# Queries of the dilated layer turned on VectorE and moved through DRAM instead of transposed on TensorE

## The chip, the cores and the metric

One NeuronCore of one Trainium2 chip runs the whole program. The metric is device time in microseconds; the kernel before takes 861.87 us (median of three runs, 861.83 to 862.84). Engines are named as the profile names them: PE is TensorE (PEld its weight loads), DVE is VectorE, ACT is ScalarE, POOL is GpSimd, SP is SyncE, whose queue starts nearly all DMAs.

## What is computed

Two layers on x of 512 tokens by 1024 features, float32. Each: RMS norm, one input projection, attention in 16 heads of 64, a SiLU gate, an output projection, a residual add. Layer A attends in three groups of dilation per head, merged by their softmax denominators; layer B attends in a neighbourhood of a token grid.

```python
def mixer_a(hn, w_in, w_out, q_gain, k_gain, t5_bias):
    proj = hn @ w_in
    qkv = proj[..., :n_qkv].reshape(b, s, N_DIL_GROUPS, 3, N_HEADS, HEAD_DIM)
    gate = proj[..., n_qkv:]
    for g, (window, dilation) in enumerate(DILATED_PAIRS):
        q = rms_norm(qkv[:, :, g, 0], q_gain[g])
        k = rms_norm(qkv[:, :, g, 1], k_gain[g])
        v = qkv[:, :, g, 2]
        o, lse = dilated_group_attention(q, k, v, t5_bias[...], dilation, reach)
    alpha = jax.nn.softmax(jnp.stack(lses), axis=0)
    y = jnp.sum(alpha[..., None] * jnp.stack(outs), axis=0)
    return (y * jax.nn.silu(gate)) @ w_out
```

Layer A's scores need queries and keys with the head's features on the partitions; the projection leaves them with tokens on the partitions. So they have to be transposed.

## The kernel before

Products in float32 are made of three matmuls each: a value is split into a high part (`wh`, `hn_h`, `q0h`, `k0h`) and a low part (`wl`, `hn_l`, `q0l`, `k0l`), and `mm3` adds high by high, high by low and low by high. Weights come from DRAM in loads of 512 KB (`wraw`, three buffers, line 175). ScalarE casts the high part of 512 columns (`wh`, line 127), VectorE or GpSimd subtracts (`wl`, line 131); four buffers of each, so a split runs four weight tiles ahead. A weight tile feeds 12 matmuls of 512 columns.

Layer A is worked in eight chunks `hc` of two heads. `main_a` issues, per chunk, the projection `rawk` (keys and values of groups 1 and 2; eight weight tiles, 96 matmuls), `rawq` (queries of all groups and key of group 0; 96 matmuls), the values of group 0 (`v0_a`, 24) and the gate (`gate_a`, 24). Each projection lands in four PSUM banks (`acc`), which ScalarE takes out scaled (line 428); GpSimd squares, VectorE sums, a reciprocal root is computed, VectorE scales (line 284; for `rawq` held back until after the gate's product, line 458).

The attention of a chunk is a side stream laid between the projections of the next chunk. TensorE's order is written by the program (`manual_schedule`): `run` alternates the main stream with the side stream, and a side step is emitted when an estimated clock passes a due time (`yield 1200`, `yield "wait", key, delay`). The other engines' orders are made by a planner from the same program. `later_on` puts DMA starts at due times of the same clock, and `keep_in_program_order` fixes them in SP's queue. SP waits in order: a DMA that waits for data or for a buffer holds all behind it.

Per chunk, the side stream is: `k_a` (two groups of four 128x128 transposes, line 210), `q_a` (four groups: queries of the three groups of dilation and the key of group 0), `v_a` (one), then `attn_a`: scores `log` of half the tokens (u = 0), the products with v of the chunk before (`weigh`, tile `o`, called through `pending`), scores of the other half (u = 1). The probabilities are turned by VectorE in 32x32 blocks (`turner.put`, line 636) and sent through DRAM in 256 KB pieces (`td` written at line 645, `pt` read at line 649).

In TensorE's order, counted in projection matmuls from the start of the next chunk's `rawk`: q groups at 24, 30, 36 and 42, the `vt` group at 48, scores at 60, products `o` at 72, end of `rawk` at 96, second scores at 129, k groups at 165 and 171, end of `rawq` at 192.

Of the kernel before, what the change touches and what calls it, by code (L numbers as in the profile page):

```python
# [13 lines left out]
F32 = mybir.dt.float32  # L14
# [28 lines left out]
def tile_hybrid_encoder(  # L43
# [44 lines left out]
    make_identity(nc, ident)  # L88
    ones = cp.tile([P, S], F32R, name="ones")
    nc.vector.memset(ones.bitcast(F32), 1.0)  # L90
# [174 lines left out]

    def squares(raw, ss, i, ns):
        sq = wk.tile([P, 512], F32, tag="sq", name="sq")[:, : ns * 64]
        nc.gpsimd.tensor_mul(sq, raw[:, i, : ns * 64], raw[:, i, : ns * 64])  # L268
# [6 lines left out]
    def head_norm(raw, ss, ns, held):  # L275


        rs = wk.tile([P, 32], F32, tag="rs", name="rs")
        rsqrt(nc.vector if ns == 8 else nc.gpsimd, rs[:, : 4 * ns], ss[:, : 4 * ns], 4 * ns, 1.0 / DH)

        def scale():
            for i in range(4):
                v = raw[:, i, : ns * 64].rearrange("p (a b) -> p a b", b=64)
                m = nc.vector.tensor_mul(
                    v, v, rs[:, i * ns : (i + 1) * ns].unsqueeze(2).to_broadcast([P, ns, 64])
                )
# [58 lines left out]
    for _ in range(9):  # L345
        nc.tensor.matmul(busy, ones[:, :P], ones, start=True, stop=True)
    wsteps = steps()
# [61 lines left out]
    rk = wk.tile([P, 4608], F32, tag="rawk", name="rawk", bufs=1)  # L409

    def project_qk(n, ns, key, hc, guard, first=False, **kw):

        box = []

        def evac(i, acc):
            if not box:
                q = key == "rawq"
                if q:
                    box.append(wk.tile([P, 4, n], F32, tag="rawq", name=key, bufs=1))
                else:  # L420
                    o = 4 * n * (hc % (2 if n == 512 else 3))
# [3 lines left out]
            if first:  # L425
                nc.scalar.copy(raw[:, i, :], acc[:, :n])
                return
            nc.scalar.activation(raw[:, i, :], acc[:, :n], AF.Copy, scale=rs_n[:, i : i + 1])  # L428
            squares(raw, ss, i, ns)

        tile_of = lambda hn: lambda k, i: hn[:, k, P * i : P * (i + 1)]
        yield from project(tile_of(hn_h), tile_of(hn_l), n, evac, guard, **kw)
        raw, ss = box
        if first:
            st["first"] = raw, ss
            return
        normed(raw, ss, ns, key, hc)

    def normed(raw, ss, ns, key, hc):
        head_norm(raw, ss, ns, key == "raw" or (key == "rawq" and hc < NHC - 2))  # L440
        st[key, hc] = raw
        stamp[key, hc] = clock[0]

    def first_out():

        raw, ss = st.pop("first")
        for i in range(4):
            nc.scalar.activation(raw[:, i, :], raw[:, i, :], AF.Copy, scale=rs_n[:, i : i + 1])
            squares(raw, ss, i, 4)
        normed(raw, ss, 4, "rawk", 0)  # L450

    def gate_a(hc):
# [4 lines left out]
        eg = wk.tile([P, S], F32, tag="eg", name="eg")  # L457
        tc.keep_in_program_order(nc.vector.tensor_mul(tjr(gt), to_tjr(acc[0]), tjr(rs_half)))
        while later:
            later.pop()()  # L460
        nc.scalar.activation(eg, gt, AF.Tanh)
# [24 lines left out]
    def k_a(hc):  # L486
        yield "wait", ("rawk", hc), 12500 if hc == 0 else 16000 if hc < NHC - 1 else 10000
        k12 = wk.tile([P, 2, 512], F32, tag="k12", name="k12", bufs=1)
        raw = st.pop(("rawk", hc))
        for g in range(2):  # L490
            tp = transpose4(raw, g * P)
            nc.vector.tensor_scalar(k12[:, g, :], tp, gk[:, g + 1 : g + 2], None, op0=ALU.mult)
            yield
        st["k12", hc] = k12, raw
        stamp["k12", hc] = 0

    def q_a(hc):
        yield "wait", ("rawq", hc), 15000 if hc < NHC - 2 else 13000
        raw = st.pop(("rawq", hc))
        q0h = wk.tile([P, 512], F32R, tag="q0h", name="q0h", bufs=1)  # L500
        q0l = wk.tile([P, 512], F32R, tag="q0l", name="q0l", bufs=1)
        q12 = wk.tile([P, 2, 512], F32, tag="q12", name="q12", bufs=1)
        k0h = wk.tile([P, EXT], F32R, tag="k0h", name="k0h", bufs=1)
        k0l = wk.tile([P, EXT], F32R, tag="k0l", name="k0l", bufs=1)
        tp = transpose4(raw, 0)
# [6 lines left out]
        for g in range(2):  # L512
            tp = transpose4(raw, (g + 1) * P)
            nc.vector.tensor_copy(tjr(q12[:, g, :]), to_tjr(tp))
            yield
        st["q", hc] = q0h, q0l, q12, k0h, k0l
        stamp["q", hc] = 0

    def v_a(hc):
# [136 lines left out]
    def attn_a(hc):  # L656
        e0, e12 = st.pop(("e", hc))
        q0h, q0l, q12, k0h, k0l = st.pop(("q", hc))
        k12, v12 = st.pop(("k12", hc))
# [4 lines left out]
        def scores(u):  # L664
# [13 lines left out]
            for t, lgs, cs, n in tiles:  # L678
                for g in range(2):
                    for j in range(4):  # L680
                        c = P * t + 32 * j
                        for hd in range(2):
                            hs = slice(64 * hd, 64 * hd + 64)
                            matmul(
                                lgs[hd][32 * j : 32 * j + 32, 256 + P * g : 384 + P * g],
                                q12[hs, g, c : c + 32],
                                k12[hs, g, P * j : P * j + P],
# [41 lines left out]
        def turn_p(hd, t, pr):  # L729
# [4 lines left out]
            nc.vector.tensor_copy(dst, tp.rearrange("p (i a r) -> p i a r", i=4, a=4))  # L734

        def weigh():
            assert not any(t.left for t in turners)
            o = bank("o")
            mms = []
            for g in range(2):  # L740
                for j in range(4):
                    c = 256 + P * g
                    mms.append((
# [301 lines left out]
    def side():  # L1045
# [20 lines left out]
        for hc in range(NHC):  # L1066
            if hc < NHC - 1:
                yield from k_a(hc)
                yield from chain(q_a(hc), v_a(hc))
                yield from attn_a(hc)  # L1070
                if hc == 2:
                    bias_rows()
            else:
                gap[0] = cycle((500, 500, 700))
                yield from chain(q_a(hc), k_a(hc), attn_a(hc))
        yield from residual(xg)
# [107 lines left out]
```

## Time and profile before

| | |
|---|---|
| median of three runs | 861.87 us (861.83 to 862.84) |
| profiled execution | 863.44 us |
| its span, first to last instruction | 861.7 us |
| granted TensorE clock | 0.999 |
| busy: PE, PEld, DVE, ACT, POOL | 854.2, 712.2, 513.3, 423.1, 296.2 us |
| DMA | 128.64 MB, mean 149 GB/s |

The span is one execution; the profiled execution's own time is 1.7 us longer than its span. A row of groups reads: line, engine, operation, out<-in, shapes, count, then busy time and mean ns of one, then the idle time of the engine before these instructions and what ended it. A row of the timeline reads: start and length in us, engine, line, operation, count. A row of windows gives the busy share of each engine with its count of instructions, then TensorE's clock, the DMA share and the GB/s. A matmul's length there includes its latency; the pitch from start to start tells its cost.

### The profile page before, as it was taken

The page shows a single profiled execution, that of the slowest core. Times are in us where ns is not written, and L with a number is a line of the kernel's source. Part 1 is how long each engine was busy: PE and PEld are TensorE (multiplying, and loading weights), DVE is VectorE, ACT ScalarE, POOL GpSimd, SP SyncE. Part 2 cuts the span into 40 slices and gives each one's busy share as a digit, 9 for nine tenths or more (in the row PEclk, how much of TensorE's full clock was granted, in tenths as well). Part 3 has the DMA queues.
Part 4 walks back from the last instruction along what each step waited for, and adds up shares of the span by engine and source line. Part 5 has one row for each costly group of instructions (what it writes and reads, how often), then busy time and mean ns, then how long its engine had stood idle before and what let it go on. Part 6 is the DMA issues. An engine that isn't in the chain of part 4 may idle for free.

```text
span 861.7 us, 15492 instructions
## 1 busy us (share of the span) xinstructions
PE 854.2 (99%) x5643; PEld 712.2 (83%) x5643; DVE 513.3 (60%) x1323; ACT 423.1 (49%) x880; POOL 296.2 (34%) x493
## 2 busy tenths in 40 slices
PE   8999999999999999999999999999999999999998
PEld 6788888788788788788788788789988899889786
DVE  6445666566476566566466775538466656766642
ACT  7432653553553553553552564435466645665541
POOL 2351441441541432442342432112444335542411
PEclk9999999999999999999999999999999999999999
DMA  7343565564465464465465274265235664656223
GB/s 247 110 131 108 150 170 157 159 178 137 138 202 156 125 200 130 133 192 148 129 171 175 84 229 105 65 197 179 95 113 149 180 168 145 167 160 174 99 96 124
DMA packets 59707, 128.64 MB, mean 149 GB/s; under 512 B 6384, under 2 KB 23728, under 8 KB 59632
## 3 DMA queue, kind: packets, MB, share of 16 engines
q1 hardware_dynamic: 59344, 127.66, 49.3%
q8 instruction: 44, 0.72, 0.4%
q14 instruction: 31, 0.25, 0.1%
q10 hardware_dynamic: 288, 0.01, 0.0%
HBM read 102.82 MB, written 24.83 MB: 148 GB/s over the span
## 4 chain that ended last, share of the span: by engine, by line
PE 97%; ACT 1%; DVE 1%; DMA 1%; issue 0%; ACTq 0%; DVEq 0%
PE acc L206 82%; PE log L206 5%; PE o L206 5%; PE tp L210 4%; DMA hg<-in_head_gain 1%; ACT p L976 1%; DVE hn_l L368 0%; ACT p L564 0%; ACT rawk L428 0%; ACT wh L127 0%; PE pa L206 0%; PE pl L206 0%; PE pk L206 0%; DVE wl L131 0%; DVE pt L889 0%
## 5 line engine op out<-in xcount | busy, mean ns | idle before, releaser
L127 ACT CAST wh<-wraw 128x512 fp32r<-128x512 f32 (+1 forms) x276 | 161.6, 587 | 298.1 <-PE acc L206 247.4
L206 PE MATMUL acc<-wh,hn_h 128*128 128x512 f32 (+1 forms) x768 | 296.5, 386 | 0.8 <-ACT wh L127 0.7
L206 PE MATMUL acc<-wh,hn_l 128*128 128x512 f32 (+1 forms) x768 | 286.6, 373 | 0.0
L206 PE MATMUL acc<-wl,hn_h 128*128 128x512 f32 (+1 forms) x768 | 286.1, 373 | 0.4 <-DVE wl L131 0.4
L131 POOL TENSOR_TENSOR wl<-wraw,wh 128x512 fp32r<-128x512 f32 (+1 forms) x110 | 137.7, 1252 | 392.9 <-ACT wh L127 342.2
L131 DVE TENSOR_TENSOR wl<-wraw,wh 128x512 fp32r<-128x512 f32 (+1 forms) x166 | 113.2, 682 | 141.5 <-ACT wh L127 137.0
L206 PEld LDWEIGHTS acc<-wh,hn_h 128*128 128x128 f32 x768 | 144.6, 188 | 27.4 <-issue 5.5
L206 PEld LDWEIGHTS acc<-wh,hn_l 128*128 128x128 f32 x768 | 144.6, 188 | 21.1
L206 PEld LDWEIGHTS acc<-wl,hn_h 128*128 128x128 f32 x768 | 144.9, 189 | 19.0 <-DVE wl L131 0.9
L206 PE MATMUL acc<-hn_h,wh 128*128 128x512 f32 x192 | 76.9, 400 | 0.2
L206 PE MATMUL acc<-hn_h,wl 128*128 128x512 f32 x192 | 74.9, 390 | 0.0
L206 PE MATMUL acc<-hn_l,wh 128*128 128x512 f32 x192 | 74.8, 390 | 0.0
L725 ACT ACTIVATE p<-p,mn 128x512 f32<-128x512 f32 (+1 forms) x64 | 44.8, 700 | 53.9 <-DVE mn L714 53.9
L564 ACT ACTIVATE p<-p,mn 128x512 f32<-128x512 f32 (+3 forms) x128 | 69.1, 586 | 0.0
L269 DVE TENSOR_REDUCE ss<-sq 128x4 f32<-128x256 f32 (+1 forms) x96 | 48.4, 504 | 27.3 <-POOL sq L268 26.8
L636 DVE STREAM_TRANSPOSE tr<-p 128x512 f32<-128x512 f32 (+1 forms) x80 | 54.1, 688 | 12.1 <-ACT p L564 10.0
L268 POOL TENSOR_TENSOR sq<-rawk 128x256 f32<-128x256 f32 x64 | 40.5, 640 | 40.5 <-ACT rawk L428 33.5
L206 PE MATMUL acc<-y_h,wh 128*128 128x512 f32 x128 | 52.2, 408 | 0.0
L206 PE MATMUL acc<-y_h,wl 128*128 128x512 f32 x128 | 50.0, 390 | 0.0
L206 PE MATMUL acc<-y_l,wh 128*128 128x512 f32 x128 | 50.0, 390 | 0.0
L206 PEld LDWEIGHTS acc<-hn_h,wh 128*128 128x128 f32 x192 | 36.1, 188 | 9.8 <-ACT rawk L428 2.1
L206 PEld LDWEIGHTS acc<-hn_h,wl 128*128 128x128 f32 x192 | 36.0, 188 | 7.7
(131 smaller groups left out, 1077.8 us busy)
## 6 DMA issues: line engine op xcount, KB each, us to landing
wraw<-in_w SPq DMA_DIRECT2D x95, 512.0 KB
wraw<-in_w SPq DMA_DIRECT2D x38, 384.0 KB
td<-tr SPq DMA_DIRECT2D x56, 256.0 KB
pt<-td SPq DMA_DIRECT2D x56, 256.0 KB
td<-tr SPq DMA_DIRECT2D x24, 224.0 KB
pt<-td SPq DMA_DIRECT2D x24, 224.0 KB
e<-l_d SPq DMA_DIRECT2D x32, 112.0 KB
e<-l_d SPq DMA_DIRECT2D x16, 128.0 KB
```

Source lines behind the costliest of these rows:

```text
L127: nc.scalar.copy(h, raw)
L131: eng.tensor_sub(l, raw, h.bitcast(F32))
L206: nc.tensor.matmul(o, l, r, **kw)
L210: nc.tensor.transpose(o, i, ident)
L268: nc.gpsimd.tensor_mul(sq, raw[:, i, : ns * 64], raw[:, i, : ns * 64])
L269: nc.vector.tensor_reduce(ss[:, i * ns : (i + 1) * ns], sq.rearrange("p (a b) -> p a b", b=64), axis=AX.X, op=ALU.add)
L564: nc.scalar.activation(pr, pr, AF.Copy, scale=mn[:, 3:4])
L636: nc.vector.transpose(dst, src[:, :n].rearrange("p (i b k) -> p i b k", b=4, k=32))
L725: nc.scalar.activation(row, row, AF.Exp, bias=mn[:, 1:2], scale=-1.0, accum_out=mn[:, 2:3])
L976: nc.scalar.activation(pr[:, o : o + n], pr[:, o : o + n], AF.Exp, bias=mn[:, 0:1], scale=-1.0, accum_out=mn[:, 2:3])
```

## The change

For chunks 0 and 2 to 5 (heads 0, 1 and 4 to 11; `moved`), `q_a` no longer transposes on TensorE. The projection is taken out into a block layout, scaled, and turned in place by VectorE in 32x32 blocks (`turn_q`, four instructions). Four DMAs write the tile to DRAM (`qd`) and four read it back with features on the partitions (`qt`), in runs of 2 KB (`move_q`). `split_q` then makes the high and low parts from SBUF. Chunks 1, 6 and 7 (heads 2, 3 and 12 to 15) keep the transposes.

Around it: the scores (u = 0) of moved chunks stand at 87 instead of 60, those of chunk 0 at 99; products with v are emitted right after the end of the next `rawk` projection (`weighed`), at 99 instead of 72; values of groups 1 and 2 get a tile of their own (three buffers), keys a single one, so ScalarE takes `rawk` out in two instructions of 256 columns; the gate is copied by ScalarE before its product, and the scaling of `rawq` is not held back for it; the due times of the sends of probabilities change; `ones` shrinks to two columns that are broadcast.

In TensorE's order after the change, a chunk from 2 to 5 reads: `vt` group at 24, scores at 87, products `o` at 99, second scores at 129, k groups at 162 and 168. In SP's queue the writes and reads of `qd` and `qt` stand as: one load of weights, four writes, one load, two reads, one load, two reads (chunk 0: three reads, one load, one read).

```diff
 def head_norm(raw, ss, ns, held):
         def scale():
             for i in range(4):
-                v = raw[:, i, : ns * 64].rearrange("p (a b) -> p a b", b=64)
-                m = nc.vector.tensor_mul(
-                    v, v, rs[:, i * ns : (i + 1) * ns].unsqueeze(2).to_broadcast([P, ns, 64])
-                )
+                by = rs[:, i * ns : (i + 1) * ns].unsqueeze(2)
+                if len(raw.shape) == 4:
+                    v = raw[:, :, i, :].rearrange("p (h a f) r -> p f h a r", h=2, f=4)
+                    by = rs[:, i * ns : (i + 1) * ns].rearrange("p (f h) -> p f h", h=2)
+                    by = by.unsqueeze(3).unsqueeze(4).to_broadcast([P, 4, 2, 2, 32])
+                else:
...
+                m = nc.vector.tensor_mul(v, v, by)
...
+    moved = lambda hc: hc == 0 or 2 <= hc < NHC - 2
+    def part(n):
+        return rk[:, 1024 * n : 1024 * n + 1024].rearrange("p (i c) -> p i c", i=4)
 def project_qk(n, ns, key, hc, guard, first=False, **kw):
...
+                elif key == "rawk":
+                    box.append(part(0))
+                    st["v12", hc] = part(1 + hc % 3)
...
+            if key == "rawq" and moved(hc):
+                src = acc.rearrange("p (f a r) -> p f a r", f=4, a=4)
+                pieces = [(raw[:, :, i, :].rearrange("p (a f) r -> p f a r", a=4), src)]
+            elif key == "rawk":
+                pieces = [(raw[:, i, :], acc[:, :256]), (st["v12", hc][:, i, :], acc[:, 256:])]
...
 def normed(raw, ss, ns, key, hc):
-        head_norm(raw, ss, ns, key == "raw" or (key == "rawq" and hc < NHC - 2))
+        head_norm(raw, ss, ns, key == "raw")
+        if key == "rawq" and moved(hc):
+            turn_q(raw)
 def gate_a(hc):
-        tc.keep_in_program_order(nc.vector.tensor_mul(tjr(gt), to_tjr(acc[0]), tjr(rs_half)))
-        while later:
-            later.pop()()
+        nc.scalar.copy(tjr(gt), to_tjr(acc[0]))
+        nc.vector.tensor_mul(gt, gt, rs_half)
 def k_a(hc):
-        yield "wait", ("rawk", hc), 12500 if hc == 0 else 16000 if hc < NHC - 1 else 10000
+        yield "wait", ("rawk", hc), 12500 if hc == 0 else 18500 if hc < NHC - 1 else 10000
+    def turn_q(raw):
+        for i in range(4):
+            nc.vector.transpose(raw[:, :, i, :], raw[:, :, i, :])
 def q_a(hc):
         yield "wait", ("rawq", hc), 15000 if hc < NHC - 2 else 13000
         raw = st.pop(("rawq", hc))
+        if moved(hc):
+            move_q(hc, raw)
+            return
...
+    def move_q(hc, raw):
+        d = dr.tile([4, P, 512], F32, name="qd", tag="qd", bufs=2)
...
+        def write(a):
+            src = raw[:, 4 * a : 4 * a + 4].rearrange("p f i r -> p (f i r)")
+            tc.keep_in_program_order(nc.sync.dma_start(d[a], src))
...
+        def read(a):
+            dst = qt[32 * a : 32 * a + 32].rearrange("k t f x -> k t (f x)")
+            src = d[a].rearrange("(t k) x -> k t x", t=4)
+            tc.keep_in_program_order(nc.sync.dma_start(dst, src))
...
+        for a in range(4):
+            later_on(700 * a, partial(write, a))
+            later_on(6800 + 700 * a, partial(read, a))
+        def land():
+            yield "wait", ("rawq", hc), 27000
+            split_q(*tiles)
...
+    def split_q(q0h, q0l, qt, k0h, k0l):
+        src = qt[:, :, 3, :].rearrange("p t (j r) -> p t r j", j=4)
...
+        nc.scalar.copy(trj4(k0h), src)
+        put_k([(by_t(q0h), by_t(q0l), qt[:, :, 0, :])], 0)
+        nc.vector.tensor_sub(trj4(k0l), src, trj4(k0h.bitcast(F32)))
 def attn_a(hc):
+        def weighed():
+            yield "wait", ("rawk", hc + 1), 0
+            pending.pop(0)()
...
-                if u == 0:
-                    yield 1200
+                if u == 0 and hc:
+                    yield 600 if moved(hc) else 1200
+                elif hc == 0:
+                    yield "wait", ("rawk" if u == 0 else "rawq", 1), 0
                 elif hc < NHC - 2:
-                    yield "wait", ("rawk", hc + 1), 6500
+                    yield "wait", ("rawk", hc + 1), 10000
...
-                later_on(9000, partial(turned.send, pq[:, 2048 * u : 2048 * u + 2048], 11000, 1500))
-                if pending and u == 0:
+                later_on(7500 + 3000 * u, partial(turned.send, pq[:, 2048 * u : 2048 * u + 2048], 10500 + 1500 * u, 1500))
+                if 0 < hc < NHC - 2 and u == 0:
+                    yield from weighed()
+                elif pending and u == 0:
```

More of the change, by code (lines that the diff above doesn't have):

```diff
@@ L499, in q_a @@
         raw = st.pop(("rawq", hc))
[L500 to L504, printed above, removed]
+        if moved(hc):
+            move_q(hc, raw)
+            return
+        st["q", hc] = q0h, q0l, qt, k0h, k0l = q_tiles()
         tp = transpose4(raw, 0)
@@ L657, in attn_a @@
         e0, e12 = st.pop(("e", hc))
-        q0h, q0l, q12, k0h, k0l = st.pop(("q", hc))
+        q0h, q0l, qt, k0h, k0l = st.pop(("q", hc))
         k12, v12 = st.pop(("k12", hc))
@@ L1069, in side @@
                 yield from chain(q_a(hc), v_a(hc))
+                if moved(hc):
+                    yield from st.pop(("land", hc))
                 yield from attn_a(hc)
-                if hc == 2:
+                if hc == 1:
                     bias_rows()
```

79 lines of the change are left out of this document (57 added, 22 removed).

## The prediction

> **What bounds the kernel now.** I read the first page first, then PE's own waits, then one chunk of layer A in order of time (a chunk is two heads; the rows below are from 327 to 372 us, where one passes into the next).
>
> ```profile
> PE 854.2 (99%) x5643; PEld 712.2 (83%) x5643; DVE 513.3 (60%) x1323; ACT 423.1 (49%) x880; POOL 296.2 (34%) x493
> ...
> PE 97%; ACT 1%; DVE 1%; DMA 1%; issue 0%; ACTq 0%; DVEq 0%
> ```
> ```profile
> PE busy L346 <- DVE warm L335: 1.5, 1, 1.5
> PE acc L206 <- ACT wh L127: 0.7, 1, 0.7
> PE acc L206 <- DVE wl L131: 0.4, 1, 0.4
> PE tp L210 <- ACT p L564: 0.4, 1, 0.4
> PE o L206 <- issue: 0.3, 1, 0.3
> ```
>
> TensorE is busy 854.2 of 861.7 us, it makes 97% of the chain that ended last, and all its waits in the run sum to 3.3 us. So every step taken off TensorE shortens the run by its length, every new wait of TensorE lengthens it by its length, and work on the other engines costs nothing until TensorE meets it. The profiled execution took 863.44 us (span 861.7 and 1.7 around it); the median of the runs is 861.87. I sum against the profiled one and carry the difference over to the median.
>
> **What leaves TensorE.** Heads 0, 1 and 4 to 11, five chunks of eight, lose the four groups of four transposes `tp<-ident,rawq` each: 20 groups.
>
> ```profile
> L210 PE MATMUL tp<-ident,rawq 128*128 128x128 f32 x128 | 19.2, 272 | 0.0
> ```
> ```profile
> 328.18 0.39 PE L206 MATMUL acc<-wh,hn_h 128*128 128x512 f32 x1
> ...
> 331.58 0.39 PE L206 MATMUL acc<-wh,hn_h 128*128 128x512 f32 x1
> ...
> 333.62 0.60 PE L210 MATMUL tp<-ident,rawq 128*128 128x128 f32 x4
> ...
> 335.45 0.60 PE L210 MATMUL tp<-ident,rawq 128*128 128x128 f32 x4
> ...
> 340.95 0.60 PE L210 MATMUL tp<-ident,vt 128*128 128x128 f32 x4
> ```
>
> From 328.18 to 331.58 there are 15 projection matmuls: 0.227 us each. From one group to the next, 333.62 to 335.45, there are 1.83 us with six matmuls (1.36), so a group costs 0.47 us of TensorE's time, and 20 cost **9.4 us**. The 272 ns of the group row is a latency; four overlap. [...]
>
> **What the new route costs.** The normalised queries now go: VectorE turns 32x32 blocks (four instructions), four writes of 256 KB on SP's queue, four reads of 256 KB behind them, then ScalarE and VectorE split the result into q0h, q0l, k0h, k0l. The first scores of these heads (`log`) move from 60 to 87 matmuls after the next projection of k and v begins (its start in the chunk shown is 328.18), so TensorE reaches them at 328.18 + 87 x 0.227 + 0.47 (the `vt` transposes stay) = 348.4. Is the data there? The VectorE part:
>
> ```profile
> 327.50 0.19 DVE L116 SCALAR_TENSOR_TENSOR rs<-na,rs 128x32 f32<-128x32 f32 x1
> 328.38 0.69 DVE L458 TENSOR_TENSOR gt<-acc,rs_half 128x512 f32<-128x512 f32 x1 [0.68 <-PE acc L206]
> 328.98 2.49 DVE L284 TENSOR_TENSOR rawq<-rawq,rs 128x512 f32<-128x512 f32 x4
> 331.39 0.68 DVE L131 TENSOR_TENSOR wl<-wraw,wh 128x512 fp32r<-128x512 f32 x1
> ```
> ```profile
> L636 DVE STREAM_TRANSPOSE tr<-p 128x512 f32<-128x512 f32 x68 | 47.3, 707 | 11.9 <-ACT p L564 9.8 <-DMA pt<-td 1.4 <-POOL p L700 0.4
> ```
>
> The root ends at 327.7. The scaling no longer waits for the gate, so it ends 2.5 later, 330.2; four turns at 0.71 with a weight split (0.68) and the gate's product (0.69) between them end at 334.4. VectorE is 60% busy, and what is queued behind the turns (the gate's silu, splits four tiles ahead) has that lead. These instructions are free, 14 us of them in all, less ten copies of q12.
>
> The end of the path is on SP's queue. In the new order it reads: four writes, one load of weights, two reads, one load of weights, two reads. A load of weights cannot start before its buffer is free, and SP waits in order, so the last two reads start when the second load may. In the trace that load is this one:
>
> ```profile
> 341.15 0.62 ACT L127 CAST wh<-wraw 128x512 fp32r<-128x512 f32 x1 [3.00 <-PE acc L206]
> ```
> ```profile
> 341.90 1.29 POOL L131 TENSOR_TENSOR wl<-wraw,wh 128x512 fp32r<-128x512 f32 x1 [8.68 <-issue]
> ```
> ```profile
> 343.23 0.33 SPq L175 DMA_DIRECT2D wraw<-in_w  x1
> ```
>
> The last product of weight tile 4 frees a `wh` buffer, ScalarE casts (341.15), GpSimd subtracts (to 343.19), SP starts (343.23). In the changed order four q groups less and the `vt` group more lie ahead of it: 343.23 - 1.88 + 0.47 = 341.8. From there to 348.4 are 6.6 us for a 512 KB load, two reads of 256 KB and the split. What such a burst takes:
>
> ```profile
> 365.50 0.33 SPq L175 DMA_DIRECT2D wraw<-in_w  x1
> 365.92 1.80 SPq L649 DMA_DIRECT2D pt<-td  x3
> ```
> ```profile
> 365.50:366.50 1.00, 1.00 (x11) 0.65 (x11) 0.00 (x0) 0.00 (x0) 0.67 (x5) 1.00 0.03 8
> 366.50:367.50 1.00, 1.00 (x55) 0.90 (x54) 0.76 (x3) 0.00 (x0) 0.38 (x3) 1.00 0.73 250
> 367.50:368.50 1.00, 1.00 (x34) 0.73 (x19) 1.00 (x6) 0.00 (x0) 0.00 (x0) 1.00 0.97 315
> 368.50:369.50 1.00, 1.00 (x6) 0.81 (x5) 1.00 (x7) 0.20 (x1) 0.00 (x0) 1.00 0.98 297
> 369.50:370.50 1.00, 1.00 (x6) 0.84 (x5) 1.00 (x7) 1.00 (x3) 0.00 (x0) 1.00 1.05 268
> 370.50:371.50 1.00, 1.00 (x7) 0.81 (x6) 0.67 (x6) 1.00 (x4) 0.09 (x1) 1.00 0.86 164
> ```
>
> The last column is GB/s, which over 1 us is KB. Load and three reads are 1311 KB; 870 KB have moved by 369.5, the 1049 KB of a load and two reads by 370.2 (4.7 us after the issue), all by 371.5 (6.0). The confirmation comes after the last byte; no view shows it for one transfer, so I take 6.2, with 4.9 and 7.7 as the ends (4.9: the bytes alone; 7.7: four writes, a load and the first two reads, 2 MB started from 334.4 on, still fill the queue). The reads land at 348.0. [...]
>
> Behind the landing:
>
> ```profile
> L533 ACT ACTIVATE k0h<-tp,gk 128x512 fp32r<-128x512 f32 x8 | 5.5, 687 | 7.2 <-PE tp L210 7.2
> L506 ACT CAST q0h<-tp 128x512 fp32r<-128x512 f32 x8 | 4.6, 581 | 2.3 <-PE tp L210 2.3
> ```
> ```profile
> L507 DVE TENSOR_TENSOR q0l<-tp,q0h 128x512 fp32r<-128x512 f32 x8 | 5.5, 682 | 2.7 <-ACT q0h L506 2.7
> ```
> ```profile
> 344.25 0.36 PE L206 MATMUL log<-k0h,q0h 64*128 64x192 f32 x2
> ...
> 344.56 0.28 PE L206 MATMUL log<-k0h,q0l 64*128 64x192 f32 x2
> ```
>
> ScalarE makes k0h (0.58, now the plain copy), then q0h (0.69): 349.3, so TensorE waits 0.9 us. q0l is 0.68 behind q0h at 350.0, and the third product, 0.31 after the first, wants it at 349.6: 0.4 more. Together **1.3 us a chunk**, between 0 and 2.8 from the ends above. It recurs in heads 4 to 11, which have this order: four chunks, 5.4 us. In heads 0 and 1 the scores come 12 matmuls later (2.7 us) and only one read stands behind the load: no wait.
>
> The products with v move from behind the first scores, inside the projection, to just after its end (three matmuls into the next one). They keep their number and, by the rows of `o`, their cost. They cover something: ScalarE now takes the projection out in halves queued between the exponentials of the new scores, and TensorE has 12 matmuls, the 3.6 us of `o` and 6 more matmuls before it needs the last bank.
>
> ```profile
> 349.27 3.62 PE o L206 x48
> ```
> ```profile
> L725 ACT ACTIVATE p<-p,mn 128x512 f32<-128x512 f32 x48 | 34.2, 713 | 34.8 <-DVE mn L714 34.8
> ```
>
> That is 12 x 0.227 + 3.62 + 6 x 0.227 = 7.7 us of cover. Against it stand about 1.2 until the first exponential can start (an estimate: four of VectorE's steps), six activations at 0.71 (four exponentials, two normalisations) and six half evictions at an estimated 0.4 (a little over half of a whole one, 0.69 like k0h's): 7.9, less where they overlap. Even; I put it at nothing, up to 0.5 a chunk, and where the cover is gone 3.6 a chunk at most. The gate's extra copy on ScalarE, the smaller `ones` and 10.5 MB more traffic hide under TensorE.
>
> **Sum.** -9.4 + 5.4 = -4.0 us: 859.4 by the profiled execution, **857.9** by the median.
>
> **Rivals.** (1) The wait disappears: the burst lands 4.9 us or less after its load's issue, or the copies are quicker. For it: the load issued at 343.23, into an idle queue, has moved by 346.0.
>
> ```profile
> 344.00:345.00 1.00, 1.00 (x14) 0.75 (x12) 0.00 (x0) 0.59 (x1) 0.00 (x0) 1.00 0.63 135
> 345.00:346.00 1.00, 1.00 (x66) 0.86 (x65) 0.80 (x2) 0.03 (x1) 0.00 (x0) 1.00 0.93 381
> ```
>
> Against: the queue will not be idle, with two reads just ahead. Then -9.4: 852.5, chance 0.22. (2) Slower: the last two reads, held behind the weights, land late. From 7.3 us after the load's issue the wait is over 9.4 / 4 = 2.35 us in each of four chunks and eats the gain; from 7.7 (2.8 a chunk) it can be measured; at 8.4 (3.5) it is 14.0 against 9.4: 866.5. For it: SP's queue is one, the writes and first reads precede, and nothing in the queue can overtake. Against: 6.0 us sufficed for more bytes. Chance 0.27, its far part included: a long wait that lowers the clock.
>
> ```profile
> L346 PE MATMUL busy<-ones 128*128 128x512 f32 x9 | 4.2, 646 | 1.5 <-DVE warm L335 1.5
> L206 PE MATMUL acc<-hn_h,wl 128*128 128x512 f32 x192 | 74.9, 390 | 0.0
> ```
>
> The first nine matmuls took 646 ns where later ones take 390. Should a 3.5 us wait bring that back for nine matmuls, each chunk would pay 2.3 more, 9.2 in all: 875.7, chance 0.03. [...] (3) The wait just pays the gain back (1.9 to 2.8 a chunk): 860.2 to 863.6, chance 0.10.
>
> **Numbers.** The forecast (a wait of 0.3 to 1.9 a chunk) has 0.41; with the first rival, faster has 0.63. What a measurement of this kernel can tell from no change is about 0.2%, 1.7 us. The range goes from the first rival to the slower one's price: 852.5 to 866.0.
>
> **What would show it.** `tp<-ident,rawq` falls from 128 to 48. PE's waits get a row for `log`, released by ScalarE's q0h or VectorE's q0l, four times 1.3 us; where it is absent, the first rival holds; over 2.4 each, the second. The load ahead of the last two reads should start 6.6 us before the scores are due. A wait of `acc` for ScalarE's eviction after `o` would show the cover too thin. A wait on `wl` or `wh` would prove the lead of the weights wrong.

## The result, and the profile after

The changed kernel takes 889.85 us (median of four runs, 888.73 to 891.0) against 861.94: ratio 1.032, 95% interval 1.030 to 1.034. It is 28 us slower, and lies above the whole range predicted. The profiled execution took 889.36 us, its span 887.5.

The first page of the changed kernel, busy time, TensorE's clock in 40 slices, and the chain that ended last:

```profile
PE 853.6 (96%) x5563; PEld 710.0 (80%) x5563; DVE 513.6 (58%) x1333; ACT 431.8 (49%) x924; POOL 297.8 (34%) x493
...
PEclk9999999999899899799899999999999999999999
...
PE 86%; DMA 6%; ACT 3%; DVE 2%; POOL 1%; issue 1%; SPq 1%; ACTq 0%; POOLq 0%; DVEq 0%
```

TensorE has 80 transposes less, yet is as busy as before (853.6 against 854.2), the chain now holds 6% of DMA, and there are four dips in the clock row. TensorE's waits (total, times, longest) name the place:

```profile
PE log L206 <- ACT q0h L621: 24.3, 4, 7.6
PE acc L206 <- ACT rawk L458: 1.1, 1, 1.1
```

Four waits, one in each of the chunks with heads 4 to 11, of 6.37, 5.46, 7.62 and 4.89 us. The scores of heads 0 and 1 do not wait; the 1.1 us of the second row is theirs in another way: their k0h stands on ScalarE ahead of the eviction of k and v, waits there 2.87 us for its read, and TensorE meets the late eviction. One of the four in order of time on SP's queue, and then ScalarE's timeline for heads 0 and 1 (86 to 92 us) and for the same one of the four:

```profile
201.38 1.96 SPq L576 DMA_DIRECT2D qd<-rawq  x4
203.45 0.53 SPq L175 DMA_DIRECT2D wraw<-in_w  x1
204.09 1.08 SPq L583 DMA_DIRECT2D qt<-qd  x2
208.33 0.35 SPq L175 DMA_DIRECT2D wraw<-in_w  x1
208.73 0.90 SPq L583 DMA_DIRECT2D qt<-qd  x2
```
```profile
86.42 1.13 ACT L602 CAST k0h<-qt 128x512 fp32r<-128x512 f32 x1 [2.87 <-DMA qt<-qd]
...
88.58 3.02 ACT L458 ACTIVATE rawk<-acc,rs_n 128x256 f32<-128x256 f32 x8
...
219.68 1.06 ACT L602 CAST k0h<-qt 128x512 fp32r<-128x512 f32 x1 [7.37 <-DMA qt<-qd]
220.66 0.72 ACT L621 ACTIVATE q0h<-qt,gk 128x512 fp32r<-128x512 f32 x1
```

SP's order is the predicted one. The second load starts at 208.33; the last read is usable at 219.68, 11.35 us later. The windows (PE to POOL busy, clock, DMA share, GB/s) show how those 11 us went, and what came behind them:

```profile
209.00:210.00 1.00, 1.00 (x6) 0.84 (x5) 0.33 (x1) 0.62 (x1) 0.00 (x0) 1.00 1.08 186
...
211.00:212.00 1.00, 1.00 (x6) 0.81 (x6) 0.00 (x0) 0.31 (x1) 0.00 (x0) 1.00 1.08 193
...
214.00:215.00 1.00, 1.00 (x5) 0.56 (x3) 0.00 (x0) 0.00 (x0) 0.00 (x0) 1.00 1.05 170
...
217.00:218.00 1.00, 0.00 (x0) 0.00 (x0) 0.00 (x0) 0.00 (x0) 0.00 (x0) 1.00 0.28 84
...
219.00:220.00 1.00, 0.00 (x0) 0.00 (x0) 0.00 (x0) 0.32 (x1) 0.00 (x0) 0.94 0.08 29
220.00:221.00 1.00, 0.00 (x0) 0.00 (x0) 0.22 (x1) 1.00 (x2) 0.00 (x0) 0.50 0.01 4
...
225.00:226.00 1.00, 1.00 (x30) 0.62 (x12) 1.00 (x7) 0.01 (x1) 0.00 (x0) 0.50 0.00 0
226.00:227.00 1.00, 1.00 (x4) 0.76 (x4) 1.00 (x7) 1.00 (x3) 0.00 (x0) 0.64 0.00 0
```

The engines are full (share over 1) but move only 170 to 193 GB/s in these rows: single packets of 2 KB take 160 to 220 ns in the trace where they take 84 elsewhere. From 217 on only some engines still work; the first of the sixteen ends its part of the last read 4 us before the last, and no run here tells why these engines fall behind. Then the clock: at half from 219.9 to 226.7, which the scores and what follows them have to run through.

### The profile page after: what moved, and what is told of

The parts are those of the page before. It is cut to its first block, busy times and chain, and to the rows that moved or that the text cites. A ratio compares the mean times of both kernels' runs of the same rounds, so it can differ in the third digit from the quotient of the medians.

```text
span 887.5 us, 15473 instructions
## 1 busy us (share of the span) xinstructions
PE 853.6 (96%) x5563; PEld 710.0 (80%) x5563; DVE 513.6 (58%) x1333; ACT 431.8 (49%) x924; POOL 297.8 (34%) x493
## 4 chain that ended last, share of the span: by engine, by line
PE 86%; DMA 6%; ACT 3%; DVE 2%; POOL 1%; issue 1%; SPq 1%; ACTq 0%; POOLq 0%; DVEq 0%
PE acc L206 72%; DMA qt<-qd 5%; PE log L206 5%; PE o L206 5%; PE tp L210 3%; ACT wh L127 1%; POOL wl L131 1%; DMA pt<-td 1%; ACT p L1073 1%; ACT k0h L602 0%; DMA hg<-in_head_gain 0%; ACT rawk L458 0%; DVE hn_l L378 0%; DVE q0l L623 0%; ACT p L652 0%
```

## The experiments

All times are medians; the kernel before stood at 861.8 to 863.3 beside them. "Wait" is what TensorE waited ahead of the scores for q0h in the four chunks together; "clock" is what it lost at half clock between 60 and 600 us (busy time in half-microsecond windows times the missing share of the clock). The profiled executions of e1, e2, e3, e7, e15 and e16 lost another 1.7 us each at half clock in their first 12 us.

| run | edit against the changed kernel | us | ratio, 95% | wait | clock |
|---|---|---|---|---|---|
| after | none | 889.85 | 1.030 to 1.034 | 24.3 | 10.1 |
| e1 | reads ahead of the second load | 876.38 | 1.011 to 1.018 | 5.7 | 6.8 |
| e2 | no chunk moved | 863.76 | 1.000 to 1.002 | none | none |
| e3 | reads to 128 partitions | 868.09 | 1.005 to 1.009 | 3.4 | 3.4 |
| e4 | reads take the old copy | 886.63 | 1.023 to 1.031 | 14.9 | 9.8 |
| e5 | reads by t | 915.01 | 1.059 to 1.065 | 37.8 | 14.7 |
| e6 | e5, reads ahead | 907.72 | 1.050 to 1.054 | 29.9 | 15.4 |
| e7 | scores 6 us later | 894.18 | 1.034 to 1.039 | moved | 7.5 |
| e8 | filler in the wait | 884.93 | 1.023 to 1.030 | 0.4 | none |
| e9 | source in one piece | 890.14 | 1.031 to 1.034 | 21.3 | 10.9 |
| e10 | gather in the writes | 870.72 | 1.007 to 1.010 | 7.9 | 8.3 |
| e11 | e10, reads ahead | 864.23 | 1.001 to 1.003 | 3.4 | 1.7 |
| e12 | e11, scores 2 us later | 880.20 | 1.019 to 1.024 | 3.6 | 6.0 |
| e13 | e1, scores 2 us later | 886.68 | 1.027 to 1.031 | 7.9 | 11.2 |
| e14 | e12, o as much later, second scores as in the change | **858.33** | 0.994 to 0.997 | none | none |
| e15 | e11, split on two engines | 864.33 | 1.001 to 1.005 | 5.7 | 5.1 |
| e16 | e15, scores and o 1.4 us later | 860.38 | 0.997 to 0.999 | 4.4 | 4.8 |
| e17 | e14, o 1.4 us later still | 859.86 | 0.995 to 0.998 | 2.2 | 1.7 |

(In e15 and e16 the scores wait for k0h and k0l instead of q0h; those waits stand there.)

### Is it the moved queries at all (e2), and is it the queue's order (e1)?

```diff
-    moved = lambda hc: hc == 0 or 2 <= hc < NHC - 2
+    moved = lambda hc: False                          # e2
-            later_on(6800 + 700 * a, partial(read, a))
+            later_on(4200 + 700 * a, partial(read, a))   # e1
```

> No chunk goes through DRAM: all queries are transposed by TensorE as in the kernel before, all other edits of the change stay (products with v between projections, the eviction in halves, the gate's copy). Theory of the prediction: the rest of the change costs nothing (cover of 7.7 us against 7.9): 861.9, up to 864 with 0.5 a chunk. Rival: the four waits in the changed kernel are only part of its 27.9 us, and the rest of the change costs several us by itself: 865 to 870. The transpositions tp of rawq must be 128 again and the waits of log gone.

> The four reads come due 2.6 us earlier, so all four stand ahead of the second load of weights (order: four writes, load, four reads, load, load). Everything else is as changed. In the changed kernel the second load starts 6.7 us before the scores are due and the last read is usable 11.4 us after it, a wait of 6.1 us a chunk in four chunks, and a clock at half for some 7 us behind each. Theory Q (the reads are late because of what stands ahead of them in one queue): 2.6 MB instead of 3.1 MB are ahead of and in the last read, from 201.4 on; at the 200 GB/s that the changed kernel moved there this is 13 us, 214.4, against scores due at 215.0. With 1.1 for k0h and 0.7 for q0h the wait is 1 to 2 us, the clock stays up, and the run takes 852.5 + 4 x 1.5 + 2 = 860 us (856 to 866). Theory D (writing runs of 2 KB to 32 partitions is itself slow, the worse the more reads stand back to back): the reads take as long as before, the wait stays over 3.5 us with the clock lowered: 872 to 890.

e2 gives 863.76 beside 863.28: the rest of the change (the products with v in their new place, the eviction in halves, the gate's copy) costs 0.5 us, at most 1.6 by the interval. All of the loss lies in the moved queries. e1 takes 13 us off, so the order on SP's queue is part of the cause.

```profile
PE log L206 <- ACT q0h L621: 5.7, 4, 2.1
```

Its waits are the 1.4 us a chunk that theory Q named, but the time is 12 to 16 above what Q made of them. The clock fell in four places, with 1.7 us of work lost at each, and the first chunk's eviction came 2.0 us late. And the packets did not speed up: with only reads in flight they took 150 to 176 ns, so the reads themselves are slow.

### What makes the reads slow (e3, e4, e9)?

```diff
-            dst = qt[32 * a : 32 * a + 32].rearrange("k t f x -> k t (f x)")
-            src = d[a].rearrange("(t k) x -> k t x", t=4)
+            dst = qt[:, a].rearrange("k f x -> k (f x)")     # e3: 128 partitions
+            src = d[a]
+            src = past[a].rearrange("(t k) x -> k t x", t=4) # e4: the chunk before's copy
+            src = d[a].rearrange("(k t) x -> k t x", t=4)    # e9: 32 partitions, source in one piece
```

> Each read of 256 KB goes to 128 partitions with one run of 2 KB each instead of 32 partitions with four runs of 2 KB; same bytes, same runs, same order on the queue. It leaves the turned blocks in the wrong places, so the transposition is not delivered and the values differ. Theory D (few destination partitions make the packets slow): packets of the reads fall from 160 to 220 ns towards 84, the last read is usable 2 to 4 us earlier, the wait falls from 6 to 2 to 4 us: 862 to 876. Theory Q (queue total) and theory F (data just written to DRAM comes back slowly): unchanged, 886 to 892.

> The reads take the copy in DRAM that the chunk before wrote, not the one just written: the same traffic in the same order, the values are those of another chunk. Theory F (a read of data just written, or the wait for the write's confirmation, holds the reads): the reads start up to 2 us earlier and land so much earlier: 868 to 880. Theories Q and D: unchanged, 886 to 892, since SP issued the reads in the changed kernel without a wait for the writes behind the second load.

> Takes apart the two things that differed in the run with reads to 128 partitions: there the destination was wide and the source in one piece. Here each read still fills only 32 partitions with four runs of 2 KB, but takes its 256 KB from DRAM in one piece (row 4k+t instead of row 32t+k), which puts values in the wrong places; bytes, runs, order and due times stay. Theory D (the 32 destination partitions): packets stay at 150 to 220 ns, waits of 5 to 7 us, 886 to 892. Theory S (four source rows 64 KB apart): packets fall to 84 ns, waits of about 1 us, 864 to 870.

e3 against e9 settles it. Both take each 256 KB from DRAM in one piece; the destination differs, 128 partitions or 32, and the times are 868 and 890. (The packets differ too: with both sides in order, e9's trace has its four runs of 2 KB as one packet of 8 KB, against its expectation. They mostly take 580 to 920 ns in the burst, as long for their bytes as the 2 KB packets of the changed kernel, so the size of the packets is not what makes them slow.) TensorE's waits in e3, then in e9:

```profile
PE log L206 <- ACT q0h L621: 3.4, 4, 1.0
```
```profile
PE log L206 <- ACT q0h L621: 21.3, 4, 6.6
```

In e3 the reads' packets take 84 ns, and from 212 to 214 us the burst runs at over 320 GB/s:

```profile
212.00:213.00 1.00, 1.00 (x6) 0.83 (x5) 0.00 (x0) 0.24 (x1) 0.00 (x0) 1.00 0.83 326
213.00:214.00 1.00, 1.00 (x6) 0.82 (x5) 0.00 (x0) 0.39 (x1) 0.54 (x1) 1.00 0.88 338
```

There the last read is usable 5.7 us after the load's issue, inside the 4.9 to 7.7 that the prediction had put down. The rates are 170 to 193 GB/s with reads to 32 partitions in the changed kernel against 326 to 338 with reads to 128 in e3; why a narrow destination is slow shows in no run. e4 saves 3 us with an interval that overlaps the changed kernel's, though its profile waits 9 us less in all: data just written may cost a part of that size, not the bulk.

### Mending the destination, wrongly and rightly (e5, e6, e10, e11)

Read t can fill all 128 partitions with right values if it takes 32 rows of each of the four blocks.

```diff
+            dst = qt[:, t].rearrange("k f x -> k (f x)")
+            src = d[:, 32 * t : 32 * t + 32]                 # e5; e6 with reads due at 4200
```

> The same four reads of 256 KB, cut the other way: read t takes the 32 rows of each of the four blocks and fills all 128 partitions with 2 KB each, so that the same values arrive in the same places; writes, bytes, runs of 2 KB, due times and SP's order stay. Each read now needs all four writes. The run before with reads to 128 partitions (which put the values elsewhere) had waits of 0.85 + 0.3 us a chunk and 868 us. Theory D (32 partitions per read make the packets slow): as there, packets of 84 ns, last read usable 5.5 to 6 us after the second load's issue, 866 to 870. Rival (all four writes must have landed before the first read starts; that costs what the wider destination brings): first read 2 us later, waits of 2 to 3 us, 872 to 880.

> The reads cut to 128 partitions and, besides, all four due ahead of the second load of weights (four writes, load, four reads, load). The first read waits for the four writes (landed at 205.9 in the changed kernel), the reads then move 1 MB at over 300 GB/s and end by 210 to 211, and the two copies for k0h and q0h (1.1 and 0.7) end by 213, before the scores are due at 215. If queue order and destination are the whole of the delay, no wait is left, the clock stays up, and the run takes the before time less 9.4: 853 to 855, ratio 0.990. If a wait remains for another reason (the SP queue held by the first read keeps a load late, q0l, the eviction), it is 857 to 862.

Both theories missed: 915 and 908 us. Windows of e5 with such reads alone in flight:

```profile
226.00:227.00 1.00, 0.00 (x0) 0.00 (x0) 0.00 (x0) 0.00 (x0) 0.00 (x0) 1.00 0.26 100
227.00:228.00 1.00, 0.00 (x0) 0.00 (x0) 0.00 (x0) 0.00 (x0) 0.00 (x0) 0.61 0.26 98
```

The packets are quick now (84 ns), but a quarter of the engines works: share 0.26, 100 GB/s. Each read's completion comes from four engines. The source's outermost dimension is 4, and the transfer was split by it: e3's reads, with the same destination and 128 as the outermost dimension of the source, came from all sixteen. The changed kernel's reads, with 32, came from sixteen too: of its last read the first engine ends its part at 215.61 us, the last at 219.58.

So the gather has to stand where the outermost dimension is 32, in the writes:

```diff
+        d = dr.tile([P, 4, 512], F32, name="qd", tag="qd", bufs=2)
+            src = raw[32 * t : 32 * t + 32].rearrange("k (a f) i r -> k a (f i r)", a=4)
+            dst = d[:, t].rearrange("(a k) x -> k a x", a=4)          # write t
+            dst, src = qt[:, t].rearrange("k f x -> k (f x)"), d[:, t]  # read t
```

> The gather moves from the reads to the writes: write t takes 32 partitions with four runs of 2 KB and spreads them over the copy in DRAM, read t then fills 128 partitions with one run of 2 KB each. Same bytes, runs, due times and order; the values arrive where the change puts them. The outermost of a transfer's dimensions is 32 for the writes and 128 for the reads, so all 16 engines should take part (with an outermost dimension of 4 each transfer ran on four engines only, 100 GB/s, 915 us). Theory D (few partitions as destination are slow; as source they need not be): writes as fast as now, reads with 84 ns packets, waits of 0.85 + 0.3 us in four chunks, 864 to 870. If few partitions are as slow as a source: writes at 160 to 220 ns land 3 to 4 us later, the reads wait for them, and the wait is 3 to 5 us: 876 to 886.

> As the run with the gather in the writes, and all four reads ahead of the second load of weights. If the writes are not slowed, they land at about 206, the reads run from there at over 300 GB/s to 210, the two copies end by 212.5, before the scores are due at 215: no wait, clock up, 863 less 9.4 = 853 to 856, ratio 0.990. If the writes are slowed by 3 to 4 us: the reads end at 213 to 214, the copies at 216, waits of 1 to 2 us with the clock lowered: 862 to 870. The reads wait for the writes at the head of SP's queue, so a load of weights behind them may also come late: then acc waits for wh.

e10 stands at 870.72, e11 at 864.23. The writes pay some of it: in e10, taken from 32 partitions and scattered over DRAM, they ran at 172 to 262 GB/s with packets of mostly 160 ns and landed at 207.4, where those of the changed kernel, started 0.6 later, had landed at 206.0. The reads then run at 330 to 395 GB/s:

```profile
201.00:202.00 1.00, 1.00 (x6) 0.83 (x5) 1.00 (x3) 0.23 (x1) 0.00 (x0) 1.00 0.90 172
...
209.00:210.00 1.00, 1.00 (x6) 0.83 (x5) 0.69 (x1) 0.08 (x1) 0.00 (x0) 1.00 1.11 395
```

### What a wait costs besides its length (e8)

```diff
+            if hc:
+                fill = bank("fill")
+                for _ in range(26):
+                    nc.tensor.matmul(fill, wide(P), wide(S), start=True, stop=True)
             split_q(*tiles)
```

> The changed kernel with 26 matmuls of 512 columns that nobody reads (26 x 0.227 = 5.9 us) put ahead of the first scores in the four chunks that wait. They take nothing away from the path and lie in the wait. If the wait's cost is its length alone, the run stays at 890 (888 to 893, a little more in the chunk that waits 4.9). If the clock that falls behind the wait costs besides (estimated 2.65 us a chunk from 5.3 us of work done at half speed), it falls by 8 to 10: 879 to 883, with PEclk at 1.00 through the scores.

4.9 us less, although TensorE has 23.6 us more to do: the clock row shows no dip, and the wait for q0h is all but gone.

```profile
PE log L206 <- ACT q0h L625: 0.4, 1, 0.4
```

The gain is half of what was expected. Filler of 5.9 us is longer than two of the waits it replaces (5.46 and 4.89), and what it is too long is paid. The start counts besides. In e8's profiled execution the first projection matmuls follow each other at 0.43 us until 13.2 us; in the changed kernel's the pitch is 0.23 from 7 us on:

```profile
11.06 0.63 PE L206 MATMUL acc<-wh,hn_h 128*128 128x512 f32 x1
11.48 0.63 PE L206 MATMUL acc<-wl,hn_h 128*128 128x512 f32 x1
```
```profile
10.91 0.39 PE L206 MATMUL acc<-wl,hn_h 128*128 128x512 f32 x1
11.13 0.39 PE L206 MATMUL acc<-wh,hn_l 128*128 128x512 f32 x1
```

So e8 comes to its first transposes 3.2 us later (58.65 against 55.46 us), before anything that the edit touches, and still ends 6.2 us earlier (883.19 against 889.36): 9.4 us in the rest of the run, inside the 8 to 10 that were expected, for one execution of each. Over the profiled executions of all runs this start differs by up to 3.2 us, so differences of 1 or 2 us between single profiles mean little.

### Can TensorE simply ask later (e7, e12, e13, e14, e17)?

```diff
-            yield "wait", ("rawq", hc), 27000
+            yield "wait", ("rawq", hc), 33000        # e7; 29000 in e12, e13, e14, e17
-                    yield "wait", ("rawk", hc + 1), 10000
+                    yield "wait", ("rawk", hc + 1), 16000   # e7; 12000 in e12, e13
             yield "wait", ("rawk", hc + 1), 0        # weighed: 2000 in e14, 3400 in e17
```

> The changed kernel's slow reads as they are, but the scores of heads 4 to 11 and the products with v behind them are due later: TensorE has 27 more projection matmuls (6.1 us) ahead of the scores. If the landing is only late against its consumer, the waits of 4.9 to 7.6 us fall to 0 to 1.5, and the run takes 854 to 860. Rival: what is later in the chunk (transposes of p, the next k transposes, the turned p of the next scores) now comes late instead and waits 2 us or more: 862 to 875.

```profile
PE acc L206 <- ACT rawk L458: 28.6, 5, 7.7
PE o L206 <- PE log L206: 2.9, 4, 0.7
```
```profile
223.38 1.07 ACT L602 CAST k0h<-qt 128x512 fp32r<-128x512 f32 x1 [9.24 <-DMA qt<-qd]
...
225.49 3.01 ACT L458 ACTIVATE rawk<-acc,rs_n 128x256 f32<-128x256 f32 x8
```

The wait changed its name and grew. ScalarE works in order here: k0h sits at its head for 9.24 us waiting for the read, and behind it, from 225.49 on, stand the evictions of k and v, for which TensorE's next projection waits (7.5 us in this chunk). So the scores may move only as far as the end of that projection, 9 matmuls or 2.0 us.

> As the run with the gather in the writes and the reads ahead of the second load (864 us: waits of 0.85 + 0.3 us and scores drawn out by 0.9 us in four chunks), with the scores of heads 4 to 11 due 9 matmuls (2.0 us) later, still ahead of the eviction of k and v on ScalarE, so that this does not queue behind k0h. Theory of the whole: the change's gain of 9.4 is there and was eaten by late data alone; with the data in place 0 to 0.5 us after it is due the run takes 854 to 857 (ratio 0.990 to 0.993). Rival: something else in the change costs several us when TensorE does not wait (evictions of k and v behind the scores' exponentials, o with less cover): waits of acc for ScalarE's rawk appear and the run stays at 861 or more.

> The change's own writes and reads (32 partitions a read), with the reads ahead of the second load (872 to 878 us: waits of 1.4 + 0.3 us and the clock lowered) and the scores due 2.0 us later, nothing else. If lateness is all, the waits fall from 1.7 to about 0.3 and the clock holds: 856 to 861. If the slow packets hold the loads of weights as well, the next loads come late and acc waits for wh, or the landings shift with the chunk's own order and 1 us of wait remains with the clock lowered: 862 to 870.

Both got slower than without it (880 against 864, 887 against 876). Timeline of TensorE in e12:

```profile
220.83 1.18 PE L206 MATMUL log<-k,qt 64*32 64x128 f32 x64
221.94 0.50 PE L206 MATMUL acc<-wh,hn_h 128*128 128x512 f32 x1
222.28 0.39 PE L206 MATMUL acc<-wl,hn_h 128*128 128x512 f32 x1
222.51 0.40 PE L206 MATMUL acc<-wh,hn_l 128*128 128x512 f32 x1
226.17 1.97 PE L206 MATMUL o<-pt,rawk 128*64 128x128 f32 x32 [3.27 <-issue]
```

o waits 3.27 us, and e13's o waits in the same way (10.2 us in all). Of the 12 matmuls that stand between scores and o in the change, three are left; the prediction had counted them as cover for the eviction, not for o. What o waits for shows on VectorE, in the same run:

```profile
225.59 0.48 DVE L801 CUSTOM_DVE_ANT_1 p<-log,e,mn 128x256 f32<-128x256 f32 x1
```

This is the second and last reading of the first scores' bank. It ends at 226.07, and o starts 0.10 us later; in the other chunks of e12 and in all four of e14 it is 0.1 us as well. The four banks of `log` are all that their pool has (`ps_side`), and `o` takes the one that comes free. e14 moves o along, and leaves the second scores, which come behind o, where the change has them:

> The gather in the writes, the reads ahead of the second load, the scores of heads 4 to 11 due 2.0 us later as in the run that gave 880 us, but now the products with v move along, so that 12 projection matmuls stay between scores and o as in the change, and the second scores stay where they were. In the 880 us run TensorE did not wait for the data in two chunks of four and waited 3.3 us ahead of o in each. If o waited there for a bank that VectorE must first read out (its 12 matmuls of cover were cut to 3), that wait goes: 854 to 859. If it waited for the turned p or the v rows behind it on a queue, it stays: 870 to 880.

```profile
PE o L206 <- issue: 3.4, 3, 1.2
...
PE o L206 <- PE acc L206: 0.8, 1, 0.8
...
PE log L206 <- DVE q0l L623: 0.2, 1, 0.2
```

858.33 us, 3.65 below the kernel before: the fastest version, and its four executions (857.96 to 860.86) lie below all 23 of the kernel before that ran beside them (861.04 to 863.59). No wait for q0h is left, and the clock stays up from 12.7 us on. What still stands ahead of o, 0.8 to 1.2 us in each chunk, went with six more matmuls of cover:

> The 858 us run with 18 projection matmuls instead of 12 between the scores and o in heads 4 to 11; nothing else moves. There TensorE still waits 1.1 to 1.2 us ahead of o in three of four chunks, with the clock at full. Theory: this is the read-out of the scores' banks, and 6 matmuls (1.4 us) cover it: the 4.2 us of waits of o go, 854 to 855.5. Rival: o then waits for the same time at its new place or the second scores come late (15 matmuls left between o and them): 857 to 860.

```profile
PE log L206 <- ACT q0h L621: 2.2, 2, 1.2
...
PE log L206 <- DVE q0l L623: 0.6, 2, 0.3
```

o no longer waits for it, but 2.8 us of waits for q0h and q0l and 1.7 us of clock are back, and the time is the same within the intervals (859.86). Why q0h is late again in two chunks stays open.

### Shortening what lies behind the landing (e15, e16)

```diff
-        put_k([(by_t(q0h), by_t(q0l), qt[:, :, 0, :])], 0)
+        nc.vector.tensor_scalar(by_t(q0h), qt[:, :, 0, :], gk[:, 0:1], None, op0=ALU.mult)
+        # q0l as before, but behind q0h and ahead of k0l on VectorE
+        # e16 besides: 28000 for 27000 in land, 1500 for 0 in weighed
```

> The 864 us run (gather in the writes, reads ahead of the second load, due times as in the change) with q0h made by VectorE beside ScalarE's k0h instead of behind it on ScalarE. Its reads are usable 1.4 us before the scores start and the two copies (1.1 and 0.7) are what remains of the wait. The first scores can then start 0.6 to 0.7 us earlier, q0l and k0l 0.4 earlier: waits of 0.85 + 0.3 fall to 0.2 + 0.2 and the run to 860 to 862. If the landing and not the copies sets the wait: 863 to 865.

> The same with the scores of heads 4 to 11 due 6 matmuls (1.4 us) later and o moved along. No wait is left if the landing stays where it is (213.8 in the first of these chunks against scores due at 216.5, with 1.1 for k0h): 853 to 857, ratio 0.990 to 0.995. If the landing moves with the due time, since later scores make the turned p of the chunk before late and its transfers stand ahead of these, 1 us of wait remains: 859 to 866.

e15 gained nothing: VectorE now holds k0l behind q0h and q0l, and the scores wait for that instead.

```profile
PE log L206 <- DVE k0l L608: 4.9, 4, 1.3
PE log L206 <- DVE wl L131: 1.6, 1, 1.6
```

e16, with both edits, is 860.38: later scores help, the split does not.

## Why the prediction was wrong

**The landing term failed.** The prediction took a load and two reads to be usable 6.2 us after the load's issue, 4.9 to 7.7 at the ends; it was 11.35, and the wait came out at 6.1 a chunk instead of 1.3. The price was read from a burst of one load and three `pt` reads, which also go to 32 partitions, as an average from its start. For that burst 6.2 was near: in the trace of the kernel before, the load and the first two reads are usable at 371.80, 6.3 us after the load's issue, and the third read at 372.52, 0.47 us behind its last packet. The row that spoke against it stood in the quoted fence, its last: 164 GB/s at a share of 0.86, when the load was through and only narrow transfers were left (their packets take 162 ns there, in the trace of the kernel before). Here four narrow reads and two loads ran into each other, and all of them went at about that pace: 170 to 270 GB/s from 206 to 217 (mean 207), 2.3 MB, then 2.5 us with only some engines at work. e3 against e9 shows that the destination is the cause, and e3's landing that the term would have held for wide reads. In the prediction's sum four times 1.3 are 5.2, not 5.4.

**The copies were mis-sized too.** k0h takes 1.06 us, not 0.58: it now reads the key in steps through SBUF; q0h, read there in order, takes 0.72. That the steps are the cause is the author's estimate from these two. That is 0.5 us a chunk, 2 us in all.

**The clock was a tail of 3 in 100.** It came in all four chunks, and costs 10.1 us, near the 9.2 that the far part of the second rival had. The agreement is luck: the 9.2 are nine matmuls a chunk at the pace of the start, and what came were stretches of 6.8 to 10.2 us at half clock. Its condition was wrong too: the prediction asked for a wait of 3.5 us, a limit that no run shows; waits of 0.8 and 1.0 us sufficed in e3, of 1.2 and 1.3 us in e1.

**The sum with what was measured,** against e2's profiled 863.74: +24.3 of waits, +10.1 of clock, +0.7 for all other waits, -1.7 since e2's execution ran at half clock from 7.6 to 11.0 us and the changed kernel's did not, and -8.2 for the transposes. That gives 25.2; the changed kernel's 889.36 is 25.6 over it. The 8.2 are TensorE's busy time less what the clock cost: 853.4 - 1.7 = 851.7 in e2, 853.6 - 10.1 = 843.5 in the changed kernel. So this term, too, was put too high, at 9.4; why the pitch of one group did not hold for all is open.

**What held.** The groups of the changed kernel show the transposes of `rawq` that are left:

```profile
L210 PE MATMUL tp<-ident,rawq 128*128 128x128 f32 x48 | 7.2, 272 | 0.0
```

48 of 128, as predicted. The second load starts 6.7 us ahead of the moment at which TensorE runs out (208.33 to 215.06), 6.6 predicted. The cover for the eviction sufficed (no wait of acc behind o in these chunks); that o itself needs the 12 matmuls, for its bank, the prediction had not seen (e12). The course was the second rival's: the reads held behind weights landed late (11.35 us after the load's issue), and the clock fell behind the wait (10.1 us lost in four chunks).

**What stays open.** e14 gains 3.65 us of the 9.4. Its profile, of the slowest of its executions (860.86), is 2.7 us shorter than e2's (spans of 859.1 and 861.8): TensorE's busy time is 6.6 less (846.8 against 853.4), although its start costs 1.1 more (first transposes at 58.22 against 57.11 us), and its waits are 3.8 more, nearly all ahead of o (4.2 against 0.3). So the work saved is about 7.7 us, near the 8.2 above, and the waits ahead of o eat half of it. Where the rest of the 9.4 is, the profile does not say.

## What to carry to other kernels

Price a transfer by how many partitions it fills (170 to 193 GB/s to 32 in the changed kernel, 326 to 338 to 128 in e3) and by its outermost dimension (100 GB/s with 4 in e5), and price each kind of a mixed burst by itself: an average over a burst that begins with wide loads hides the narrow reads behind them. A wait of TensorE costs its length and, in most of these runs, the clock behind it (24.3 us of waits and 10.1 of clock in the changed kernel), so here a little slack ahead of a consumer was worth more than a little work saved. When a consumer is moved later, look at what stands behind it on its engine (ScalarE's evictions in e7, for which TensorE waited 28.6 us) and at the cover that is used up on its other side (o in e12, 3.27 us).

## What was not expected of the hardware

The clock falls in pieces of one length. Between 60 and 600 us the half-clock stretches that the windows of these runs show are 3.41 (e3, e15), 6.83 (the changed kernel at 219.88 us) or 10.24 us long (the changed kernel at 363.24, e9), multiples of 3.41. They begin at no fixed distance from the wait, 2.9 to 4.8 us after its start in the changed kernel; from one to the next there (219.88, 291.56, 363.24, 438.34) are 71.68, 71.68 and 75.10 us, 21, 21 and 22 times a third of 10.24. What sets these steps shows in no run. In e3 the waits of 0.80 and 0.98 us drew one of 3.41 each, those of 0.79 and 0.87 none; behind all four stand narrow score matmuls and a stall of 0.30 to 0.31 us. Which of several such waits draws the clock down differs from run to run (the first and the third in e3, the second alone in e11), and the scatter of the runs goes with it: e16's executions with a granted clock of 1.000 took 857.97 and 858.31 us, those with 0.992 to 0.994 took 863.23 to 866.02.

Slow reads also slow what shares the engines with them: where loads and narrow reads ran together in the changed kernel (209 to 212 us), the 4 KB packets of the loads took 340 to 390 ns (medians of each microsecond); in e3, beside wide reads, 160 to 200 (208 to 213 us).
